# Decoder step: layer 1's window scores on fp32 tiles of 32 rows, values projected second, and the sample's mixing on 128 rows

## The chip, the cores and the metric

The kernel runs on one core of a Trainium2 chip. The metric is the device time of one execution in microseconds. Three runs of the kernel before took 1108.77, 1109.03 and 1109.35 us; their median is 1109.03.

## The reference

One inference step of a two-layer decoder for 256 prompt tokens and 8 sample sequences of 8 tokens, 320 tokens in all, with a model width of 1024. Layer 0 runs a gated MLP whose mixing matrix works along the positions, and a retention mixer. Layer 1 runs a sliding-window attention of 16 query heads on 4 key heads with RoPE and a learned sink for each head. Each layer then has a cross attention into 256 memory tokens and a squared-ReLU MLP. Cut to what the change touches:

```python
def sgu_mix(u, v, ln_g, ln_b, w_s, b_s):          # layer 0; c = 128 (prompt) or 8 (sample)
    vn = layer_norm(v, ln_g, ln_b)
    w = jnp.where(tril, w_s[:, :c, :c], 0)
    mixed = einsum('gts,bnsgd->bntgd', w, vn by chunks) + b_s[:, :c]
    return u * mixed

q, k, v = split(h @ w_qkv + b_qkv)                # layer 1; q and k through rotary
s = einsum('...qkgd,...skd->...kgqs', q, k) * 64 ** -0.5
s = where(valid, s, -inf)                         # 0 <= distance < 128
p = softmax(concatenate([s, sink]))[..., :-1]
o = einsum('...kgqs,...skd->...qkgd', p, v)
```

All is computed in float32.

## The kernel before

Activations are feature-major: 8 chunks of 128 features by 320 tokens. Weights stream from memory in tiles of 128 x 2048, in the order of a list, `_plan`. To keep float32 accuracy in the one-pass fp32r form of a matmul, weights and activations are split into a rounded high part and the rest: ScalarE makes `whi`, VectorE makes `wlo` (1024 columns each, four buffers), and `gemm2` runs three matmuls for each product: high by high, high by low, low by high. `gemm_tok` does the same with tokens as output rows, 48 matmuls and, for the sample, 16 more. The split of the weight after next is issued when a projection begins.

Work that isn't a projection is put between the matmuls of projections by hand: `hook(i, f, j=7)` runs `f` at step `j` of 16 of the i-th projection from now, and TensorE takes its instructions in that order. VectorE's and ScalarE's order comes from the scheduler of the framework.

Layer 1 before. The projection `w_qkv` has the groups 4 (keys), 0 to 3 (queries; a group holds one query head for each of the four key heads), and 5 (values, token-major). `qk_group` evicts a group: VectorE multiplies by the row scale and forms the four rotary products, POOL adds them into `QA`. A key head's half-heads lie on 32 of the 128 rows of `QA`. For scores the kernel stacks: `hilo` splits keys and queries into high and low parts, `stack_k` (into a tile tagged `k8b`) and `stack_q` (into one tagged `Z`) copy 32-row pieces so that one key head's high and low halves fill 128 rows, with 32 copies on VectorE and 32 on ScalarE. Each score block of one head is then two fp32r matmuls of 256 columns on the whole array, 64 in all.

The attention of the prompt is cut into 12 units, run by `slot`: `w1` (scores, masked maximum on VectorE, exponentials on ScalarE, normalising on VectorE), `w2f` (transposes) and `w3` (times values). Slots are hooked from the value projection on, through the four memory key projections (`mem1.mk`) and the memory value projections (`mem1.mv`); `ws_prep`, `ws_scores`, `ws_tr` and `ws_pv` do the sample's attention.

Layer 0's mixing: for each of 8 chunks the prompt's two blocks are matmuls with 128 rows, and the sample's is one with 64 rows, `VA[2]` (rows 0 to 63 of the tile `kb8`) by `wts`. Rows 64 to 127 of the same tile hold the retention values `VR[2]`; rows 64 to 127 of `wd_s` hold the retention's sample decay.

In the trace's names `mm` and `at` are PSUM banks of projections and of the rest, `k8b` and `Z` the stacked keys and queries (or `kb8` with `cst` in the mixing), `k` the tile `QA` (tag `k10`), `w` a scratch tile, `cst` the constants.

Of the kernel before, what the change touches and what calls it, by code (L numbers as in the profile page):

```python
# [9 lines left out]
F32 = mybir.dt.float32  # L10
F32R = mybir.dt.float32r
I32 = mybir.dt.int32
AF = mybir.ActivationFunctionType
ALU = mybir.AluOpType
# [3 lines left out]
P = 128  # L18
# [55 lines left out]
def decoder_step(ctx: ExitStack, tc: tile.TileContext, d, plan):  # L74
# [9 lines left out]
    def sb(shape, tag, bufs=1, dt=F32):  # L84
        cnt[0] += 1
        return pool.tile(list(shape), dt, tag=tag, bufs=bufs, name=f"{tag}_{cnt[0]}")

    def bank(kind="mm"):
        cnt[0] += 1
        return pmm.tile([P, 512], F32, tag=kind, bufs=4, name=f"{kind}_{cnt[0]}")  # L90
# [581 lines left out]
    def cec(name, i=0, n=None):  # L672
        o, w = CE[name]
        return ce[:, o + i:o + (w if n is None else i + n)]
# [45 lines left out]
    wt = cec("wt").rearrange("p (g t) -> p g t", g=4)  # L720
    wts = cec("wd_s")[:64].rearrange("p (g t) -> p g t", g=4)
    decs = cec("wd_s")[64:128]
    G.affine_select(out=wt, in_=wt, pattern=[[0, 4], [1, P]], compare_op=ALU.is_ge, fill=0.0,
# [11 lines left out]
    scT = [lnt[:, 2048:2560], k10[:, 2560:3072]]  # L735
    scS = kb8[64:128, 1024:1280]
    kz = [va[:, 2048:2560], vr[:, 2048:2560], kb8[64:128, 1280:1792]]
    qxi = cec("xi").rearrange("p (h t) -> p h t", h=4)
# [224 lines left out]
    for g in range(4):  # L963
        def evac(ps, i0=0, g=g):
            for i in range(len(ps)):
# [5 lines left out]
                for tb in range(2):  # L971
                    T.matmul(mp[:, tb * P:(tb + 1) * P], VA[tb][:, c * P:(c + 1) * P], wt[:, g], start=True, stop=True)
                T.matmul(mp[:, NPR:NT], VA[2][:, c * P:(c + 1) * P], wts[:, g], start=True, stop=True)
                mix = sb([P, NT], "t2", 1)
# [55 lines left out]
    bv = coc("bv")  # L1030
    khl = sb([P, 2, 4, 256], "k8b", 1, F32R)

    def qk_group(g):
# [16 lines left out]
        gemm2(("w_qkv", g), nm.h, nm.l, NT, evac)  # L1050

    def hilo(src, w):
        hi = sb([P, 512], "w2", W2, F32R)[:, :w]
        lo = sb([P, 512], "w2", W2, F32R)[:, :w]
        if len(src.shape) == 3:
            hi = hi.rearrange("p (g t) -> p g t", g=src.shape[1])
            lo = lo.rearrange("p (g t) -> p g t", g=src.shape[1])
        A.activation(hi, src, AF.Copy)
        V.tensor_tensor(lo, src, hi.bitcast(F32), op=ALU.subtract)
        return hi.bitcast(F32), lo.bitcast(F32)  # L1060

    def stack_k():
        for f in range(2):
            hl = hilo(QA[:, 8 + f, :NPR], NPR)
            for kv in range(4):
                r = slice(32 * kv, 32 * kv + 32)
                for x in range(2):
                    for du in range(2):
                        q = (f + 2 * du) * 32
                        if du:  # L1070
                            V.tensor_copy(khl[q:q + 32, x, kv], hl[x][r])
                        else:
                            A.activation(khl[q:q + 32, x, kv], hl[x][r], AF.Copy)

    sq_t = {}

    def stack_q(gp, fs=(0, 1)):
        if 0 in fs:
            sq = sb([P, 2080], "Z", 1, F32R)[:, :2048].rearrange("p (k g t) -> p k g t", k=4, g=2)
            sq_t[gp] = sq  # L1080
        sq = sq_t[gp]
        for f in fs:
            hl = hilo(QAv[:, 2 * gp:2 * gp + 2, f, :NPR], 512)
            for kv in range(4):
                r = slice(32 * kv, 32 * kv + 32)
                for x in range(2):
                    q = (f + 2 * x) * 32
                    if x:
                        V.tensor_copy(sq[q:q + 32, kv], hl[x][r])
                    else:  # L1090
                        A.activation(sq[q:q + 32, kv], hl[x][r], AF.Copy)

# [22 lines left out]

    units = []
    for gp in range(2):
        for pr in range(2):
            units.append((0, gp, pr, None))
        for kv in range(4):  # L1120
            units.append((1, gp, kv // 2, kv))
    us, up_, uo = {}, {}, {}

    def w1(u):
        n, gp, pr, kv = units[u]
        heads = [(k, g) for k in ((2 * pr, 2 * pr + 1) if n == 0 else (kv,)) for g in range(2)]
        nh = len(heads)
        kw = 512 // nh
        s = sb([P, 512], "w2", W2).rearrange("p (h k) -> p h k", k=kw)
        mx = sb([P, nh], "w_mx", 4)  # L1130
        msk = m1[:, P:256] if n == 0 else m1
        for j, (k, g) in enumerate(heads):
            if j % 2 == 0:
                sp = bank("at")
            o = (j % 2) * 256
            for x in range(2):
                T.matmul(sp[:, o:o + 256], sq_t[gp][:, k, g, n * P:(n + 1) * P], khl[:, x, k],
                         start=(x == 0), stop=(x == 1))
            V.tensor_tensor_reduce(out=s[:, j], in0=sp[:, o:o + kw], in1=msk, op0=ALU.add, op1=ALU.max,
                                   scale=1.0, scalar=NEG, accum_out=mx[:, j:j + 1])  # L1140
        sums = sb([P, nh], "w_sm", 4)
        if n == 0:
            for i in range(2):
                i0 = CV["sink_p"][0] - CV["sink_s"][0] + (2 * pr + i) * 4 + 2 * gp
                sink_softmax(s[:, 2 * i:2 * i + 2], 2, mx[:, 2 * i:2 * i + 2], nsink[:, i0:i0 + 2],
                             cvc("sink_p", (2 * pr + i) * 4 + 2 * gp, 2), sums[:, 2 * i:2 * i + 2], True)
        else:
            i0 = CV["sink_p"][0] - CV["sink_s"][0] + kv * 4 + 2 * gp
            sink_softmax(s, 2, mx, nsink[:, i0:i0 + 2], cvc("sink_p", kv * 4 + 2 * gp, 2), sums, True)
        us[u] = s  # L1150

    def w2f(u):
        n, gp, pr, kv = units[u]
        s = us.pop(u)
        tp = bank("at")
        pt = sb([P, 512], "w2", W2)
        for j in range(4):
            if n == 0:
                T.transpose(tp[:, j * P:(j + 1) * P], s[:, j], ident)
            else:  # L1160
                T.transpose(tp[:, j * P:(j + 1) * P], s[:, j % 2, (j // 2) * P:(j // 2 + 1) * P], ident)
        A.activation(pt, tp, AF.Copy)
        up_[u] = pt

    def w3(u):
        n, gp, pr, kv = units[u]
        pt = up_.pop(u)
        first = n == 0 or kv % 2 == 0
        if first:
            uo[n, gp, pr] = bank("at")  # L1170
        po = uo[n, gp, pr]
        for i in range(2):
            k = 2 * pr + i if n == 0 else kv
            ro = slice((k % 2) * 64, (k % 2) * 64 + 64)
            kb = 0 if n == 0 else i
            T.matmul(po[ro, :256], VW[:, kb, k * 64:(k + 1) * 64], pt[:, i * 256:(i + 1) * 256],
                     start=(n == 0 or i == 0), stop=(n == 0 or i == 1))
        if n == 0 or kv % 2 == 1:
            src = po[:, :256].rearrange("p (g q) -> p g q", g=2)
            c0 = pr * 4 + 2 * gp  # L1180
            oh = OH[:, c0:c0 + 2, n * P:(n + 1) * P]
            A.activation(oh, src, AF.Copy)
            V.tensor_tensor(OL[:, c0:c0 + 2, n * P:(n + 1) * P], src, oh.bitcast(F32), op=ALU.subtract)

# [82 lines left out]

    def slot(i):
        for u in (2 * i - 4, 2 * i - 3):
            if 0 <= u < 12:  # L1270
                w3(u)
        for u in (2 * i - 2, 2 * i - 1):
            if 0 <= u < 12:
                w2f(u)
        for u in (2 * i, 2 * i + 1):
            if u < 12:
                w1(u)

    def rows_out():
# [4 lines left out]

    qk_group(0)
    hook(0, stack_k)
    qk_group(1)
    hook(0, lambda: stack_q(0, (0,)))
    hook(1, lambda: stack_q(0, (1,)))
    qk_group(2)  # L1290
    qk_group(3)
    hook(0, lambda: slot(0))
    gemm_tok([("w_qkv", 5)], nm.h, nm.l, XS, 256, evac)
    hook(0, lambda: slot(1), rows_out)
    hook(1, lambda: slot(2), lambda: stack_q(1))
    hook(2, ws_prep, lambda: slot(3))
    hook(3, lambda: slot(4))
    for g in range(4):
        mem1.mk(g)
    hook(0, lambda: slot(5), lambda: ws_scores(0))  # L1300
    hook(1, lambda: slot(6), lambda: ws_scores(1))
    hook(2, lambda: slot(7), lambda: ws_tr(0))
    hook(3, lambda: ws_tr(1), j=3)
# [49 lines left out]
def _plan():  # L1353
# [35 lines left out]
    p += mo(0) + mlp(0)  # L1389
    p += [("w_qkv", 4), ("w_qkv", 0), ("w_qkv", 1), ("w_qkv", 2), ("w_qkv", 3), ("w_qkv", 5)]  # L1390
    p += [("w_mk", 1, g) for g in range(4)] + [("w_mv", 1, 0, 0), ("wk",), ("w_mv", 1, 0, 1), ("w_mv", 1, 1, 0),
# [205 lines left out]
```

## Time and profile before

| | |
|---|---|
| median of 3 runs | 1109.03 us |
| the profiled execution | 1110.15 us, span 1108.0, granted clock 0.995 |
| busy: PE, PEld | 1079.5 (97%), 1018.4 (92%) |
| busy: DVE, ACT, POOL | 716.3 (65%), 519.3 (47%), 98.8 (9%) |
| chain that ended last | PE 88%, DVE 6%, ACT 2%, DMA 2%, issue 1% |
| HBM traffic | 181 GB/s over the span |

PE is the matmul engine's streaming, PEld its weight loads, which overlap it. A matmul's drawn length includes its latency, so the distance between two starts tells its cost, not its length. The granted clock is in parts of full speed, and the stage of layer 1's projections and window attention lies from 607 to 725 us of the span.

### The profile page before, as it was taken

The page shows a single profiled execution, that of the slowest core. Times are in us where ns is not written, and L with a number is a line of the kernel's source. Part 1 is how long each engine was busy: PE and PEld are TensorE (multiplying, and loading weights), DVE is VectorE, ACT ScalarE, POOL GpSimd, SP SyncE. Part 2 cuts the span into 40 slices and gives each one's busy share as a digit, 9 for nine tenths or more (in the row PEclk, how much of TensorE's full clock was granted, in tenths as well). Part 3 has the DMA queues.
Part 4 walks back from the last instruction along what each step waited for, and adds up shares of the span by engine and source line. Part 5 has one row for each costly group of instructions (what it writes and reads, how often), then busy time and mean ns, then how long its engine had stood idle before and what let it go on. Part 6 is the DMA issues. An engine that isn't in the chain of part 4 may idle for free.

```text
span 1108.0 us, 18438 instructions
## 1 busy us (share of the span) xinstructions
PE 1079.5 (97%) x7424; PEld 1018.4 (92%) x7424; DVE 716.3 (65%) x1427; ACT 519.3 (47%) x894; POOL 98.8 (9%) x108
## 2 busy tenths in 40 slices
PE   7999999999999999999999979999999999999996
PEld 7888989999978999999999978889969999999995
DVE  8978866776545766454547998857445865555542
ACT  6455632654344555353436557645133554443432
POOL 4400000022000200000002131102000200000001
PEclk9999999999999999999999999999999999999998
DMA  9443358646777544444444334547587344444421
GB/s 340 158 146 124 134 190 283 235 143 234 295 294 307 224 149 153 152 153 152 153 153 153 122 114 158 175 164 277 198 309 283 120 150 150 153 153 153 152 76 48
DMA packets 30980, 201.53 MB, mean 182 GB/s; under 512 B 3624, under 2 KB 4792, under 8 KB 7992
## 3 DMA queue, kind: packets, MB, share of 16 engines
q1 hardware_dynamic: 27584, 187.13, 46.7%
q0 software_dynamic: 2512, 11.54, 2.9%
q10 hardware_dynamic: 800, 1.70, 0.5%
q8 instruction: 58, 0.95, 0.3%
q14 instruction: 26, 0.21, 0.1%
HBM read 187.51 MB, written 12.85 MB: 181 GB/s over the span
## 4 chain that ended last, share of the span: by engine, by line
PE 88%; DVE 6%; ACT 2%; DMA 2%; issue 1%; SPq 0%; ACTq 0%; DVEq 0%
PE mm L62 75%; PE at L62 13%; DVE wlo L62 2%; DMA stage<-ws 1%; DVE XL L62 1%; DVE t L62 1%; DVE w L62 1%; ACT whi L62 1%; DVE Z L62 0%; DVE X L62 0%; ACT XH L62 0%; DMA X<-x 0%; ACT w L62 0%; ACT Z L62 0%; ACT sqt L62 0%
## 5 line engine op out<-in xcount | busy, mean ns | idle before, releaser
L62 DVE TENSOR_TENSOR wlo<-stage,whi 128x1024 fp32r<-128x1024 f32 (+1 forms) x270 | 334.3, 1245 | 198.1 <-ACT whi L62 196.4
L62 ACT ACTIVATE whi<-stage 128x1024 fp32r<-128x1024 f32 (+1 forms) x270 | 280.2, 1051 | 380.2 <-PE mm L62 277.9
L62 PE MATMUL mm<-HH,whi 128*128 128x320 f32 (+1 forms) x960 | 293.7, 307 | 0.0
L62 PE MATMUL mm<-HL,whi 128*128 128x320 f32 (+1 forms) x960 | 293.0, 305 | 0.0
L62 PE MATMUL mm<-HH,wlo 128*128 128x320 f32 (+1 forms) x960 | 292.7, 305 | 0.0
L62 PE MATMUL mm<-XH,whi 128*128 128x320 f32 x912 | 286.4, 314 | 5.8 <-ACT whi L62 5.8
L62 PE MATMUL mm<-XH,wlo 128*128 128x320 f32 x912 | 283.0, 311 | 0.4 <-DVE wlo L62 0.4
L62 PE MATMUL mm<-XL,whi 128*128 128x320 f32 x912 | 282.9, 310 | 0.0
L62 PEld LDWEIGHTS mm<-HH,whi 128*128 128x128 f32 x960 | 180.1, 188 | 2.5 <-issue 1.6
L62 PEld LDWEIGHTS mm<-HL,whi 128*128 128x128 f32 x960 | 180.4, 188 | 0.4 <-DVE HL L62 0.3
L62 PEld LDWEIGHTS mm<-HH,wlo 128*128 128x128 f32 x960 | 180.3, 188 | 0.1
L62 PEld LDWEIGHTS mm<-XH,whi 128*128 128x128 f32 x912 | 172.3, 189 | 7.4 <-ACT whi L62 5.8
L62 PEld LDWEIGHTS mm<-XH,wlo 128*128 128x128 f32 x912 | 172.1, 189 | 0.9 <-DVE wlo L62 0.9
L62 PEld LDWEIGHTS mm<-XL,whi 128*128 128x128 f32 x912 | 172.4, 189 | 0.6
L62 POOL TENSOR_TENSOR ssq<-ssq,sqt 128x320 f32<-128x320 f32 x39 | 41.5, 1065 | 638.2 <-ACT sqt L62 637.2
L62 DVE TENSOR_TENSOR X<-mm,X 128x320 f32<-128x320 f32 x112 | 51.7, 488 | 57.7 <-PE mm L62 57.5
L62 DVE SCALAR_TENSOR_TENSOR t<-mm,RB 128x320 f32<-128x320 f32 x64 | 30.1, 490 | 25.5 <-PE mm L62 22.6
L62 DVE TENSOR_TENSOR HL<-t,HH 128x320 fp32r<-128x320 f32 x80 | 36.7, 485 | 10.5 <-ACT HH L62 9.9
L62 ACT ACTIVATE t<-t 128x320 f32<-128x320 f32 x80 | 34.0, 460 | 17.9 <-DVE t L62 17.9
L62 DVE SCALAR_TENSOR_TENSOR XL<-X,cv,XH 128x320 fp32r<-128x320 f32 x48 | 37.7, 808 | 4.5 <-ACT XH L62 4.5
L62 ACT ACTIVATE HH<-t 128x320 fp32r<-128x320 f32 x80 | 34.5, 462 | 11.2 <-DVE t L62 10.7
L62 ACT ACTIVATE XH<-X,cv 128x320 fp32r<-128x320 f32 x48 | 26.3, 554 | 20.6 <-DVE X L62 19.2
(232 smaller groups left out, 1076.7 us busy)
## 6 DMA issues: line engine op xcount, KB each, us to landing
stage<-ws SPq DMA_DIRECT2D x162, 1024.0 KB, 4.8
o_ret_s<-stage POOLq DMA_DIRECT2D x8, 512.0 KB, 6.1
HH<-ws SPq DMA_DIRECT2D x4, 1024.0 KB, 6.9
HL<-ws SPq DMA_DIRECT2D x4, 1024.0 KB, 6.6
k8a<-ws SPq DMA_DIRECT2D x2, 1024.0 KB, 8.8
o_mem_k<-k8a POOLq DMA_DIRECT2D x2, 1024.0 KB, 8.2
o_mem_v<-k8b POOLq DMA_DIRECT2D x2, 1024.0 KB, 11.2
cst<-ce SPq DMA_DIRECT2D x1, 1296.0 KB, 10.6
```

What stands on the lines that cost most here:

```text
L62: r = f(*a, **k)
```

## The change

It does three things. Layer 1's scores are taken from `QA` as it stands, in fp32: `w1` runs for each head and half-head four matmuls of 32 rows, one for each key head, into four PSUM banks, and then the softmax of all of them; `hilo`, `stack_k` and `stack_q` are gone. There are three batches in place of 12 units: second block with query heads 0 and 1, first block with all four, second block with 2 and 3, of 16, 32 and 16 matmuls. The values are projected right after the keys, ahead of the queries. The sample's mixing matmul runs over all 128 rows of `kb8`, with zeros in the lower half of `wts`, and the retention's decay gets a place and a load of its own.

```diff
-    wts = cec("wd_s")[:64].rearrange("p (g t) -> p g t", g=4)
-    decs = cec("wd_s")[64:128]
+    wts = cec("wd_s").rearrange("p (g t) -> p g t", g=4)
...
+    decs = kb8[64:128, 1792:2048]
+    S.dma_start(decs, d["dec_s"])
...
-                T.matmul(mp[:, NPR:NT], VA[2][:, c * P:(c + 1) * P], wts[:, g], start=True, stop=True)
+                T.matmul(mp[:, NPR:NT], kb8[:, c * P:(c + 1) * P], wts[:, g], start=True, stop=True)
...
-    def hilo(src, w):
-    def stack_k():
-    def stack_q(gp, fs=(0, 1)):
...
-            for x in range(2):
-                T.matmul(sp[:, o:o + 256], sq_t[gp][:, k, g, n * P:(n + 1) * P], khl[:, x, k],
-                         start=(x == 0), stop=(x == 1))
...
+    def w1(n, gp, tag):
+        gs = range(4) if n == 0 else (2 * gp, 2 * gp + 1)
+        kw = 512 // len(gs)
+        sp = [bank("at") for _ in range(4)]
+        for j, g in enumerate(gs):
+            for f in range(2):
+                for kv in range(4):
+                    r = slice(32 * kv, 32 * kv + 32)
+                    T.matmul(sp[kv][:, j * kw:(j + 1) * kw], QAv[r, g, f, n * P:(n + 1) * P], QA[r, 8 + f, :kw],
+                             start=(f == 0), stop=(f == 1))
+        big = sb([P, 2080 if tag == "Z" else 2048], tag)
...
+        for kv in range(4):
+            s = big[:, kv * 512:(kv + 1) * 512].rearrange("p (h k) -> p h k", k=kw)
...
+            sink_softmax(s, nh, mx, nsink[:, i0:i0 + nh], cvc("sink_p", kv * 4 + gs[0], nh), sums, True)
...
+        for kb in range(n + 1):
+            for i in range(2):
+                k = 2 * pr + i
+                T.matmul(po[i * 64:i * 64 + 64, :w], VW[:, kb, k * 64:(k + 1) * 64], pts[i][:, kb * w:(kb + 1) * w],
+                         start=(kb == 0), stop=(kb == n))
...
-    qk_group(0)
-    hook(0, stack_k)
-    qk_group(1)
-    hook(0, lambda: stack_q(0, (0,)))
-    hook(1, lambda: stack_q(0, (1,)))
-    qk_group(2)
-    qk_group(3)
-    hook(0, lambda: slot(0))
     gemm_tok([("w_qkv", 5)], nm.h, nm.l, XS, 256, evac)
-    hook(0, lambda: slot(1), rows_out)
-    hook(1, lambda: slot(2), lambda: stack_q(1))
-    hook(2, ws_prep, lambda: slot(3))
-    hook(3, lambda: slot(4))
+    hook(2, lambda: w1(1, 0, "k8b"), j=9)
+    hook(3, lambda: w2f(1, 0, 0), lambda: w2f(1, 0, 1), j=9)
+    hook(4, lambda: w3(1, 0, 0), lambda: w2f(1, 0, 2), lambda: w2f(1, 0, 3), rows_out, j=3)
+    hook(4, lambda: w1(0, 0, "Z"), j=13)
+    hook(5, lambda: w3(1, 0, 1), ws_prep, j=5)
+    hook(6, lambda: w2f(0, 0, 0), lambda: w2f(0, 0, 1), j=3)
+    hook(6, lambda: w3(0, 0, 0), lambda: w2f(0, 0, 2), lambda: w2f(0, 0, 3), j=13)
+    hook(7, lambda: w3(0, 0, 1), j=3)
+    hook(7, lambda: w1(1, 1, "k8b"), j=9)
+    for g in range(4):
+        qk_group(g)
     for g in range(4):
         mem1.mk(g)
...
-    p += [("w_qkv", 4), ("w_qkv", 0), ("w_qkv", 1), ("w_qkv", 2), ("w_qkv", 3), ("w_qkv", 5)]
+    p += [("w_qkv", 4), ("w_qkv", 5), ("w_qkv", 0), ("w_qkv", 1), ("w_qkv", 2), ("w_qkv", 3)]
...
-    w8[64:] = ce.pop("dec_s").reshape(64, 4, 64)
...
+        "dec_s": ce.pop("dec_s"),
```

Where the first scores stand on TensorE before: inside the value projection (`mm` from `whi`, `XH`), which follows query group 3. `x2` are the two matmuls of a head.

```order
L62 MATMUL mm_6594<-whi_6509,XH_5893 128x256
L62 MATMUL mm_6594<-wlo_6510,XH_5893 128x256
L62 MATMUL mm_6594<-whi_6509,XL_5894 128x256
L62 MATMUL at_6632<-k8b_6128,Z_6456 128x256 x2
L62 MATMUL at_6639<-k8b_6128,Z_6456 128x256 x2
L62 MATMUL at_6671<-k8b_6128,Z_6456 128x256 x2
L62 MATMUL at_6678<-k8b_6128,Z_6456 128x256 x2
L62 MATMUL mm_6593<-whi_6513,XH_5893 128x256
```

And in the change: behind 30 matmuls of query group 2. Each row is one fp32 matmul of 32 rows for another key head, from `QA` (`k`) alone, and three more such rounds of four follow.

```order
L62 MATMUL mm_6475<-XH_5894,whi_6396 128x320
L62 MATMUL mm_6475<-XL_5895,whi_6396 128x320
L62 MATMUL mm_6475<-XH_5894,wlo_6397 128x320
L62 MATMUL at_6506<-k_917_6128 128x256
L62 MATMUL at_6507<-k_917_6128 128x256
L62 MATMUL at_6508<-k_917_6128 128x256
L62 MATMUL at_6509<-k_917_6128 128x256
```

So the first scores moved from the value projection, then the last of the six, into query group 2, now the fifth of the six.

VectorE ahead of its first score rows (`ISA` is the masked maximum) before: the split of queries into `w`, a weight split, the copies into `Z`, and then the eviction of query group 3.

```order
L62 TENSOR_TENSOR w_995_6544<-k_917_6127,w_994_6543 128x512
L62 TENSOR_TENSOR wlo_6599<-stage_6596,whi_6598 128x1024
L62 CAST Z_6456<-w_995_6544 32x512 x4
L62 TENSOR_TENSOR t_996_6579<-mm_6517,RB_6240 128x320
L62 TENSOR_TENSOR t_997_6580<-mm_6518,RB_6240 128x320
L62 SCALAR_TENSOR_TENSOR t_998_6583<-t_996_6579,cv_62,cst_6122 128x320
L62 SCALAR_TENSOR_TENSOR t_999_6584<-t_997_6580,cv_62,cst_6122 128x320
L62 SCALAR_TENSOR_TENSOR t_1000_6588<-t_996_6579,cv_62,cst_6122 128x320
L62 TENSOR_TENSOR wlo_6603<-stage_6596,whi_6602 128x1024
L62 SCALAR_TENSOR_TENSOR t_1001_6589<-t_997_6580,cv_62,cst_6122 128x320
L62 ISA w_1010_6630,w_mx_6631<-at_6632,cst_6122 128x128
L62 ISA w_mx_6631 128x1
```

In the change there is no copy: the eviction of group 1 (`t`), two weight splits, and the maxima, which now write into the tile tagged `k8b`.

```order
L62 SCALAR_TENSOR_TENSOR t_972_6454<-t_970_6450,cv_62,cst_6123 128x320
L62 SCALAR_TENSOR_TENSOR t_973_6455<-t_971_6451,cv_62,cst_6123 128x320
L62 SCALAR_TENSOR_TENSOR t_974_6459<-t_970_6450,cv_62,cst_6123 128x320
L62 TENSOR_TENSOR wlo_6471<-stage_6464,whi_6470 128x1024
L62 SCALAR_TENSOR_TENSOR t_975_6460<-t_971_6451,cv_62,cst_6123 128x320
L62 TENSOR_TENSOR wlo_6622<-stage_6619,whi_6621 128x1024
L62 ISA k8b_6526,w_mx_6527<-at_6506,cst_6123 128x256
L62 ISA w_mx_6527 128x1
```

Behind group 1's eviction the maxima of a whole batch stand in one block, ahead of the eviction of group 2.

## Rows read from the trace of the kernel before

**Rows 1.** stretches of the layer 1 projections and window attention: busy us of each engine, granted clock:

```profile
640.00:660.00 20.00, 14.41 (x93) 13.71 (x93) 19.76 (x33) 9.27 (x13) 5.58 (x6) 0.91 0.29 106
...
sum 118.00, PE 110.19 PEld 102.45 DVE 105.62 ACT 74.50 POOL 23.39; mean PE 22.04 PEld 20.49 DVE 21.12 ACT 14.90 POOL 4.68
```

**Rows 2.** timeline of PE, 692 to 694 us (start, us, engine, operation, count):

```profile
692.76 1.46 PE L62 MATMUL at<-k8b,Z 128*128 128x256 f32 x10
694.05 0.28 PE L62 MATMUL mm<-HH,whi 128*128 128x256 f32 x1
694.17 0.27 PE L62 MATMUL mm<-HL,whi 128*128 128x256 f32 x1
```

**Rows 3.** timeline of PE around the first scores, with idle time and its releaser:

```profile
653.73 2.12 PE L62 MATMUL at<-k8b,Z 128*128 128x256 f32 x8 [3.83 <-DVE Z L62]
655.65 0.41 PE L62 MATMUL mm<-whi,XH 128*128 128x256 f32 x1
655.87 0.41 PE L62 MATMUL mm<-wlo,XH 128*128 128x256 f32 x1
...
659.79 0.39 PE L62 MATMUL at<-k8b,Z 128*128 128x256 f32 x1 [1.10 <-DVE w_mx L62]
```

**Rows 4.** timeline of PE, three later waits of the stage:

```profile
646.81 0.35 PE L62 MATMUL mm<-whi,XH 128*128 128x256 f32 x1 [0.66 <-DVE t L62]
...
670.45 0.51 PE L62 MATMUL at<-k8b,Z 128*128 128x256 f32 x2 [1.06 <-DVE w_mx L62]
...
691.40 0.48 PE L62 MATMUL at<-k8b,Z 128*128 128x256 f32 x2 [0.91 <-DVE Z L62]
```

**Rows 5.** timeline of DVE ahead of the first scores:

```profile
651.26 1.87 DVE L62 TENSOR_TENSOR wlo<-stage,whi 128x1024 fp32r<-128x1024 f32 x1
653.17 1.78 DVE L62 CAST Z<-w 32x512 fp32r<-32x512 f32 x4
```

**Rows 6.** groups of DVE from 607 to 726 us: the copies into stacked tiles (count | busy, mean ns):

```profile
L62 DVE CAST Z<-w 32x512 fp32r<-32x512 f32 x16 | 6.7, 420 | 0.4
...
L62 DVE CAST k8b<-w 32x256 fp32r<-32x256 f32 x16 | 4.5, 319 | 0.1
```

**Rows 7.** PE, fp32 on the whole array: a group of the span, and the timeline at 712 us:

```profile
L62 PE MATMUL at<-k8a,k 128*128 128x256 f32 x64 | 15.4, 386 | 0.4 <-ACT w L62 0.4
...
712.78 0.66 PE L62 MATMUL at<-stage,XH 128*128 128x128 f32 x4
713.28 0.56 PE L62 MATMUL at<-k,XH 128*128 128x64 f32 x4
713.68 0.55 PE L62 MATMUL at<-stage,XH 128*128 128x128 f32 x3
```

**Rows 8.** PE, column tiles: the timeline at 146 us, and weight loads from 140 to 150:

```profile
146.09 1.07 PE L62 MATMUL at<-stage,Z 128*32 128x256 f32 x16
147.09 0.75 PE L62 MATMUL at<-k8a,w 128*128 128x256 f32 x4
...
L62 PEld LDWEIGHTS at<-cst,HH 128*128 128x128 f32 x4 | 0.6, 190 | 0.0
...
L62 PEld LDWEIGHTS at<-stage,Z 128*32 128x32 f32 x16 | 0.4, 109 | 0.6 <-issue 0.4
```

**Rows 9.** timeline of PE: the sample's mixing pair on 64 rows:

```profile
117.05 0.43 PE L62 MATMUL at<-cst,k8b 64*128 64x64 f32 x2
117.41 0.71 PE L62 MATMUL at<-cst,HH 128*128 128x128 f32 x4
```

**Rows 10.** timeline, all engines: the end of a query group and its rotation:

```profile
645.69 0.31 PE L62 MATMUL mm<-XL,whi 128*128 128x320 f32 x1
...
645.84 0.31 PE L62 MATMUL mm<-XH,wlo 128*128 128x320 f32 x1
646.18 0.89 DVE L62 TENSOR_TENSOR t<-mm,RB 128x320 f32<-128x320 f32 x2
...
650.82 1.24 POOL L62 TENSOR_TENSOR k<-t,t 128x320 f32<-128x320 f32 x1 [1.62 <-DVE t L62]
```

More of the change, by code (lines that the diff above doesn't have):

```diff
@@ L1030, in decoder_step @@
     bv = coc("bv")
-    khl = sb([P, 2, 4, 256], "k8b", 1, F32R)
     def qk_group(g):
@@ L1050, in qk_group @@
         gemm2(("w_qkv", g), nm.h, nm.l, NT, evac)
-    def hilo(src, w):
[L1053 to L1060, printed above, removed]
-    def stack_k():
[L1063 to L1066, printed above, removed]
-                for x in range(2):
[L1068 to L1075, printed above, removed]
-    def stack_q(gp, fs=(0, 1)):
[L1078 to L1091, printed above, removed]
     isc = 0.125
@@ L1114, in sink_softmax @@
             V.tensor_scalar(s[:, h], s[:, h], sums[:, h:h + 1], None, op0=ALU.mult)
[L1116 to L1119, printed above, removed]
-        for kv in range(4):
[L1121 to L1136, printed above, removed]
-                T.matmul(sp[:, o:o + 256], sq_t[gp][:, k, g, n * P:(n + 1) * P], khl[:, x, k],
-                         start=(x == 0), stop=(x == 1))
[L1139 to L1150, printed above, removed]
@@ L1152, in w2f @@
-    def w2f(u):
-        n, gp, pr, kv = units[u]
-        s = us.pop(u)
+    us, up_, uo = {}, {}, {}
+    def w1(n, gp, tag):
[9 more added lines that the diff above has]
+        big = sb([P, 2080 if tag == "Z" else 2048], tag)
+        msk = m1[:, P:256] if n == 0 else m1
+        nh = len(gs)
+        for kv in range(4):
+            s = big[:, kv * 512:(kv + 1) * 512].rearrange("p (h k) -> p h k", k=kw)
+            mx = sb([P, nh], "w_mx", 4)
+            for j in range(nh):
+                V.tensor_tensor_reduce(out=s[:, j], in0=sp[kv][:, j * kw:(j + 1) * kw], in1=msk, op0=ALU.add,
+                                       op1=ALU.max, scale=1.0, scalar=NEG, accum_out=mx[:, j:j + 1])
+            sums = sb([P, nh], "w_sm", 4)
+            i0 = CV["sink_p"][0] - CV["sink_s"][0] + kv * 4 + gs[0]
+            sink_softmax(s, nh, mx, nsink[:, i0:i0 + nh], cvc("sink_p", kv * 4 + gs[0], nh), sums, True)
+            us[n, gp, kv] = s
@@ L1155, in w2f @@
+    def w2f(n, gp, kv):
+        s = us.pop((n, gp, kv))
         tp = bank("at")
@@ L1162, in w2f, with w3 @@
         A.activation(pt, tp, AF.Copy)
[L1163 to L1183, printed above, removed]
+        up_[n, gp, kv] = pt
+    def w3(n, gp, pr):
+        po = bank("at")
+        ng = 4 if n == 0 else 2
+        w = ng * P
+        pts = [up_.pop((n, gp, 2 * pr + i)) for i in range(2)]
+        for kb in range(n + 1):
[3 more added lines that the diff above has]
+                         start=(kb == 0), stop=(kb == n))
+        src = po[:, :w].rearrange("p (g q) -> p g q", g=ng)
+        c0 = pr * 4 + 2 * gp
+        oh = OH[:, c0:c0 + ng, n * P:(n + 1) * P]
+        A.activation(oh, src, AF.Copy)
+        V.tensor_tensor(OL[:, c0:c0 + ng, n * P:(n + 1) * P], src, oh.bitcast(F32), op=ALU.subtract)
     sm_ = {}
@@ L1266, in evac @@
         V.scalar_tensor_tensor(VW[64:128, 2], fs, nm.rs[64:128, 2:3], bv[64:128], op0=ALU.mult, op1=ALU.add)
[L1268 to L1277, printed above, removed]
     def rows_out():
@@ L1283, in rows_out @@
         G.dma_start(d["wv_n"], VW[64:128, 2])
-    qk_group(0)
-    hook(0, stack_k)
-    qk_group(1)
-    hook(0, lambda: stack_q(0, (0,)))
-    hook(1, lambda: stack_q(0, (1,)))
-    qk_group(2)
-    qk_group(3)
-    hook(0, lambda: slot(0))
-    gemm_tok([("w_qkv", 5)], nm.h, nm.l, XS, 256, evac)
-    hook(0, lambda: slot(1), rows_out)
-    hook(1, lambda: slot(2), lambda: stack_q(1))
-    hook(2, ws_prep, lambda: slot(3))
-    hook(3, lambda: slot(4))
+    gemm_tok([("w_qkv", 5)], nm.h, nm.l, XS, 256, evac)
+    hook(2, lambda: w1(1, 0, "k8b"), j=9)
[9 more added lines that the diff above has]
+        qk_group(g)
     for g in range(4):
         mem1.mk(g)
-    hook(0, lambda: slot(5), lambda: ws_scores(0))
-    hook(1, lambda: slot(6), lambda: ws_scores(1))
-    hook(2, lambda: slot(7), lambda: ws_tr(0))
+    hook(0, lambda: ws_scores(0), j=5)
+    hook(1, lambda: w2f(1, 1, 0), lambda: w2f(1, 1, 1), j=1)
+    hook(1, lambda: w3(1, 1, 0), lambda: w2f(1, 1, 2), lambda: w2f(1, 1, 3), lambda: ws_scores(1), j=9)
+    hook(2, lambda: w3(1, 1, 1), lambda: ws_tr(0))
     hook(3, lambda: ws_tr(1), j=3)
```

## Prediction

> **What bounds the kernel now.** I read the page's chain first: by the table above TensorE holds 88% of it, so a microsecond is won only where TensorE stands idle, runs at the low clock, or streams something that can be streamed in less time. The table by stretches then says where that is. From 607 to 725 us, the layer 1 projections and window attention, TensorE is busy for 110.19 of 118 us while VectorE is busy for 105.62, and the stretch 640 to 660 has a granted clock of 0.91 [rows 1]. Everywhere else the waits of TensorE are small, so I went through this stage matmul by matmul.
>
> The timeline of TensorE shows the stalls. Plain matmuls of 256 columns start 0.12 us apart (694.05 to 694.17), though each is drawn 0.28 us long [rows 2]. Ahead of the first scores TensorE idles 3.83 us for VectorE's copies into the stacked query tile; the 8 scores that follow take 1.92 us (653.73 to 655.65) instead of 8 x 0.12, and 8 matmuls behind them start 0.22 us apart [rows 3]. That is 256 columns at 1.2 GHz and not at 2.4: the idle time cost the clock as well. Four more waits stand in the stage: 1.10 behind the first, and 0.66, 1.06 and 0.91 us, all for VectorE [rows 3, 4]. The reason stands in VectorE's own order: the copies that the first scores wait for begin at 653.17, behind a weight split of 1.87 us and without a gap [rows 5].
>
> **The change part by part.** *Stalls that lose their cause.* The five idle times sum to 3.83 + 1.10 + 0.66 + 1.06 + 0.91 = 7.56 us. An idle time is counted from the drawn end (0.28) and not from the next possible start (0.12), so each hides 0.16 more: 8.4 us. The 8 slow plain matmuls add 8 x 0.10 = 0.8. The change deletes the copies behind them: 32 on VectorE, 6.7 and 4.5 us busy [rows 6], with as many on ScalarE and the six hi/lo splits ahead of them. VectorE loses at least 11.2 of 105.62 us, so the order that made it late is gone.
>
> *The old scores.* 64 matmuls: 8 in 1.92 us, the other 56 at the pace of the ten at 692.76, 1.29 / 10 = 0.13 us, so 7.2. Removed: 9.1 us [rows 2, 3].
>
> *The new scores.* The operands are now fp32 and not fp32r, and an fp32 matmul of the program is two records in the trace: the 32 score matmuls of the two cross attentions stand there as 64 [rows 7]. So 16 + 32 + 16 = 64 matmuls are 128 records, 64 of 256 columns and 64 of 128. On the whole array such a record takes 15.4 / 64 = 0.24 us for 256 columns and 0.125 for 128 (712.78 to 713.28, four) [rows 7]. Run singly that would be 23 us; all depends on whether four tiles of 32 rows run side by side. No row tile has a neighbour in this trace. Column tiles do: 16 records of 128 rows by 32 columns, with 256 columns streamed, take 1.00 us, 0.0625 each, so four ran at once and one tile took 0.25 per record [rows 8]. A column tile's load has 32 columns and lasts 109 ns, a row tile's has 128; a load of 128 columns lasts 190 [rows 8]. If a tile doesn't hide its own load, a record costs 0.25 + 0.081 = 0.33 per tile, 0.083 with four tiles, and 0.10 less per tile, or 0.058, for 128 columns. 64 x 0.083 + 64 x 0.058 = 9.0 us. Low end: loads cost nothing more than the column tiles' own, 64 x 0.0625 + 64 x 0.0375 = 6.4. High end with overlap: one load at a time. The records of 64 columns (713.28 to 713.68, 0.10 each) are shorter streams than their loads and give that pace [rows 7]: 128 x 0.10 = 12.8. I take 9.0, because the half-height pair below behaves like a tile that waits for its own loads.
>
> There is a rule against this change here. The Trainium skill, "TensorE: Matmul & The Clock Gate", section on LDWEIGHTS, says that a load of 32 rows by 128 columns takes as long as one of 128 by 128, its columns divided by 1.2 GHz. The 190 ns against 109 agree that columns count. By the page's figure, as an estimate, 128 loads one after another are 13.7 us, and the sum below would end near 1105.
>
> *Drains.* The sample's 64-row pair takes 0.36 us (117.05 to 117.41) for two records of 64 columns that on the full array take 0.10 each [rows 9, 7]: a visit to another tile height costs some 0.16 us. Three batches of scores are three visits; with four tiles to fill I take 0.3 each, 0.9 in all (0.5 to 1.5).
>
> *The sample's mixing on 128 rows.* Eight such pairs now stay in the full array: 0.36 - 0.20 = 0.16 each, 1.3 us, in a stage where TensorE has no wait of note. The lower 64 rows of the weight tile are zero, so they add nothing. Between no gain and 2 us, since the matmuls around it could also lose a refill. The new 64 KB load stands in SP's queue behind a weight load and well ahead of its reader; nothing waits for it. POOL's select covers 128 rows and not 64; it is off the path.
>
> *The second-place value projection.* Its 64 matmuls are the same. It fills the time in which VectorE makes the norm's row scale, and its own results now come long before attention wants them. No cost.
>
> *What is late next.* The first batch stands behind 30 of the 48 matmuls of query group 2, at 0.15 us each some 4.4 us after the group before it ends. In the kernel before, a group's last rotation ends on POOL at 652.06, 5.9 us after VectorE began on it at 646.18 [rows 10]. The batch begins with group 0's 16 records, 1.3 us, and has 8 records of group 1's first half after them, so the last quarter of it is reached about when POOL is done. The transposes stand 7 us and more behind each batch; VectorE needs for a batch some 8 us beside the 6 us of a projection's evictions and splits, so it falls behind by about that, and catches up over the memory projections. I charge 1.0 us of new waits (0 to 3) over three batches. The normalised scores, transposes and value matmuls are the same in number and streamed columns; I cost them at nothing.
>
> **Sum.** 8.4 + 0.8 + 9.1 + 1.3 - 9.0 - 0.9 - 1.0 = 8.7 us gained. The profiled execution took 1110.15 us (span 1108.0); the sum was made in it and would bring it to 1101.5. It stands 1.1 above the median of the runs, 1109.03, so the forecast for the median is **1100.3**. With the low price of scores and drains and no new waits the gain is 12.7 us (1096.3); with the high prices (12.8, 1.5, 3.0 and no gain in mixing) it is 1.0 (1108.0), but these don't come together: the dear loads alone make 4.9 (1104.1).
>
> **The rivals.** *Loads in single file.* The scores take 12.8 us: 1104.1. For it: all loads have 128 columns, and the 64-column records show loads setting the pace [rows 7]. Against: the tiles' rows are disjoint. *VectorE stays the late one.* The whole of a batch's softmax arrives at once, between the evictions of a projection; if the transposes or a weight split then wait as long as today, the 8.4 us come back less the 1.0 I charge: 1107.7. For it: VectorE is still at some 90 of 108 us. *The other side: row tiles do not overlap.* Then 128 records run singly, 23 us with hidden loads, 64 x 0.33 + 64 x 0.23 = 36 without: 1114 to 1127, slower. It decides from 17.7 us for the scores, 0.14 per record. For it: no two row tiles run together in this trace, and the pair of 64 rows pays for its loads. Against: column tiles overlap fourfold [rows 8], and each key head has a PSUM bank of its own. *The change doesn't do what it says*, the stalls being owed to the weight splits alone: then they move and only 9.1 - 9.9 + 1.3 remains, about no change.
>
> **How the numbers follow.** The forecast's own pace 0.52 (1097.5 to 1102.5); loads that hide better, down to 1096, 0.12; single file 0.18; VectorE late 0.08; no overlap 0.07; doesn't do what it says 0.03. The range 1095.5 to 1106 takes the first three. A measurement of this kernel can tell about 0.2%, 2.2 us, from no change. Faster by more than that: the first three and a part of the late VectorE, 0.86; within it 0.07; slower 0.07.
>
> **What would show it.** In the new profile the stretch from 607 us should be about 7 us shorter, without an idle time over 1 us ahead of scores, with a clock of 1.00 throughout; records of a 32-row tile should start about 0.06 to 0.08 us apart; mixing records of 64 columns about 0.10. Records 0.10 apart whatever their columns mean single file; 0.2 and more mean no overlap. A long wait for VectorE ahead of a transpose or of a memory projection means that the load moved and did not go.

## The result and the profile after

The changed kernel takes 1095.62 us (median, 1094.03 to 1096.85) against 1109.19 for the kernel before: ratio 0.9875, 95% interval 0.9863 to 0.9886. The gain is 13.6 us where 8.7 were forecast; 0.9875 of 1109.03 is 1095.2, just under the low end of the range (1095.5). The direction and the mechanism held, the size of the gain did not. The profiled execution has a span of 1094.4 us against 1108.0.

The page of the changed kernel, the first rows of its parts 1 and 4, shows that TensorE is still what bounds:

```profile
PE 1072.5 (98%) x7480; PEld 1011.3 (92%) x7480; DVE 695.1 (64%) x1371; ACT 498.3 (46%) x850; POOL 103.3 (9%) x108
...
PE 84%; DVE 7%; DMA 5%; ACT 2%; issue 1%; POOL 1%; SPq 0%; ACTq 0%; DVEq 0%
```

The same view by stretches as [rows 1] (us, then busy us of PE, PEld, DVE, ACT, POOL with counts, granted clock, DMA share, GB/s), now for the changed kernel:

```profile
640.00:660.00 20.00, 20.00 (x166) 18.74 (x165) 18.69 (x57) 11.51 (x30) 8.77 (x6) 1.00 0.30 106
660.00:680.00 20.00, 19.06 (x200) 17.01 (x199) 16.38 (x76) 12.61 (x45) 6.78 (x11) 1.00 0.35 112
607.00:715.00 108.00, 107.06 (x848) 97.98 (x846) 85.07 (x255) 56.24 (x143) 27.32 (x28) 1.00 0.46 155
```

TensorE is busy for 107.06 of 108 us, VectorE for 85.07 instead of 105.62 of 118, and the clock of 0.91 has become 1.00. TensorE's timeline of the changed kernel shows all of the new scores, with the one wait that is left:

```profile
641.64 0.31 PE L62 MATMUL mm<-XH,wlo 128*128 128x320 f32 x1
641.88 2.01 PE L62 MATMUL at<-k 32*128 32x256 f32 x32
643.82 0.41 PE L62 MATMUL mm<-XH,whi 128*128 128x320 f32 x1
...
661.59 1.84 PE L62 MATMUL at<-k 32*128 32x128 f32 x56
664.37 0.50 PE L62 MATMUL at<-k 32*128 32x128 f32 x8 [0.94 <-POOL k L62]
664.80 0.39 PE L62 MATMUL mm<-HH,whi 128*128 128x256 f32 x1
...
685.99 2.01 PE L62 MATMUL at<-k 32*128 32x256 f32 x32
```

32 records of 256 columns take 1.94 us (641.88 to 643.82), 0.061 each, so four row tiles do run side by side. The 3.83 us ahead of scores [rows 3] and the four waits behind it [rows 3, 4] are gone; 0.94 us for POOL's rotation of the last query group is new. The weight loads, as the group of PEld from 607 to 732 us has them (busy us, mean ns | idle before), overlap each other:

```profile
L62 PEld LDWEIGHTS at<-k 32*128 32x128 f32 x128 | 5.0, 185 | 1.7 <-POOL k L62 1.1 <-issue 0.2
```

128 loads of 185 ns are 23.7 us one after another, yet PEld is busy with them for 5.0.

Where the time went is read from one landmark to the next, the last rows of the norm ahead of the stage and the first of the output projection behind it. Kernel before:

```profile
614.81 0.72 PE L62 MATMUL at<-ones,ssq 128*128 128x1 f32 x6
...
745.23 0.31 PE L62 MATMUL mm<-HH,whi 128*128 128x320 f32 x1
```

Changed kernel:

```profile
612.61 0.72 PE L62 MATMUL at<-ones,ssq 128*128 128x1 f32 x6
...
731.48 0.31 PE L62 MATMUL mm<-HH,whi 128*128 128x320 f32 x1
```

The stage takes 118.9 us instead of 130.4: 11.5 won here. The other 2.2 stand ahead of it (614.81 against 612.61). The sample's mixing lies there, from the first mixing records to the first plain matmul behind the last. Its timeline now begins and ends so:

```profile
116.43 0.61 PE L62 MATMUL at<-cst,HH 128*128 128x128 f32 x4
116.88 0.33 PE L62 MATMUL at<-cst,k8b 128*128 128x64 f32 x2
117.05 0.66 PE L62 MATMUL at<-cst,HH 128*128 128x128 f32 x4
117.55 0.33 PE L62 MATMUL at<-cst,k8b 128*128 128x64 f32 x2
117.69 0.39 PE L62 MATMUL mm<-XH,whi 128*128 128x320 f32 x1
...
150.80 0.40 PE L62 MATMUL mm<-HH,whi 128*128 128x320 f32 x1
```

In the kernel before, the first records, the second pair with the next plain matmul, and the end stand here:

```profile
116.52 0.61 PE L62 MATMUL at<-cst,HH 128*128 128x128 f32 x4
...
118.06 0.43 PE L62 MATMUL at<-cst,k8b 64*128 64x64 f32 x2
118.42 0.42 PE L62 MATMUL mm<-XH,whi 128*128 128x320 f32 x1
...
153.52 0.42 PE L62 MATMUL mm<-HH,whi 128*128 128x320 f32 x1
```

The pair takes 0.17 us where [rows 9] has 0.36, and the four records behind it 0.50 (117.05 to 117.55) where they took 0.65 (117.41 to 118.06). So a visit to 64 rows cost 0.19 inside and 0.15 behind it, where more mixing follows. The eight visits with what lies between take 34.37 us (116.43 to 150.80) instead of 37.00 (116.52 to 153.52), with the same other matmuls: 2.6 us, 0.33 a visit. The landmark's 2.2 is less sure: from the mixing's end to the norm the same matmuls take 461.3 us in the kernel before and 461.8 in the changed one, and from 459.2 to 461.8 over all traces below.

### The profile page after: what moved, and what is told of

The parts are those of the page before. It is cut to its first block, busy times and chain, and to the rows that moved or that the text cites. A ratio compares the mean times of both kernels' runs of the same rounds, so it can differ in the third digit from the quotient of the medians.

```text
span 1094.4 us, 18448 instructions
## 1 busy us (share of the span) xinstructions
PE 1072.5 (98%) x7480; PEld 1011.3 (92%) x7480; DVE 695.1 (64%) x1371; ACT 498.3 (46%) x850; POOL 103.3 (9%) x108
## 4 chain that ended last, share of the span: by engine, by line
PE 84%; DVE 7%; DMA 5%; ACT 2%; issue 1%; POOL 1%; SPq 0%; ACTq 0%; DVEq 0%
PE mm L62 74%; PE at L62 10%; DMA stage<-ws 5%; DVE wlo L62 3%; ACT whi L62 1%; DVE XL L62 1%; DVE t L62 1%; DVE X L62 0%; ACT XH L62 0%; DVE k8b L62 0%; DMA X<-x 0%; DVE Z L62 0%; POOL k L62 0%; POOL XH L62 0%; ACT sqt L62 0%
## 5 line engine op out<-in xcount | busy, mean ns | idle before, releaser
L62 DVE TENSOR_TENSOR wlo<-stage,whi 128x1024 fp32r<-128x1024 f32 (+1 forms) x270 | 330.5, 1233 | 200.8 <-ACT whi L62 199.2
```

The lines of the kernel that those rows point to most:

```text
L62: r = f(*a, **k)
```

## The experiments

Three sets of kernels, each with the kernel before (1109.11, 1108.47 and 1108.74 us) on the same chip; the changed kernel went with the second and third as `changed_again` (1094.45 us, ratio 0.9874 [0.9857, 0.989]) and `changed_thrice`.

**Do the tiles overlap because their matmuls alternate?** `tiles_in_turn` only moves the loop over key heads outward, so that each tile's matmuls follow one another:

```diff
-        for j, g in enumerate(gs):
-            for f in range(2):
-                for kv in range(4):
+        for kv in range(4):
+            for j, g in enumerate(gs):
+                for f in range(2):
```

> The changed kernel with the same 64 score matmuls in another order: key head outermost, so that neighbours on TensorE use the same 32-row tile. Theory A (four tiles run side by side, and each hides its loads): neighbours now queue, a record costs 0.23 us for 256 columns and 0.125 for 128, 64 of each make 22.7 us in place of some 6, so about 16 us more than the changed kernel, 1112. If a tile can't hide its own load: 0.33 and 0.23, 36 us, about 1125. Rival (the tiles' neighbours don't matter, a record of 32 rows is simply cheap): no change, 1095 to 1096.

Measured: 1108.04 us, ratio 0.9988 [0.9979, 0.9997]. Nearly the whole gain is lost, though less than with loads that nothing hides. Its TensorE timeline, its loads and its stretch:

```profile
640.33 4.91 PE L62 MATMUL at<-k 32*128 32x256 f32 x32
645.17 0.41 PE L62 MATMUL mm<-XH,whi 128*128 128x320 f32 x1
...
669.95 0.41 PE L62 MATMUL mm<-HL,whi 128*128 128x256 f32 x1
670.16 0.41 PE L62 MATMUL mm<-HH,wlo 128*128 128x256 f32 x1
```

```profile
L62 PEld LDWEIGHTS at<-k 32*128 32x128 f32 x128 | 14.7, 187 | 1.2 <-issue 0.2
```

```profile
660.00:680.00 20.00, 20.00 (x165) 18.98 (x164) 15.82 (x75) 11.41 (x42) 4.91 (x9) 0.91 0.30 107
```

The batch takes 4.84 us instead of 1.94, 0.151 a record, and PEld is busy for 14.7 us instead of 5.0: the loads of one tile in this batch start 0.22 us apart, where the changed kernel's loads of four tiles start within 0.02 us of each other. Behind the second batch (6.6 us, a tile at a time) 11 plain matmuls start 0.21 us apart, the pace of 1.2 GHz, though TensorE had not waited: the clock was lost as well. Of the 12.1 us that the stage takes longer than in `changed_again`, 9.5 are the scores', 1.3 the plain matmuls' at this clock, and most of the rest is a later wait of 1.1 us for ScalarE.

The starts of single records say two things more. Within one tile records of 256 columns start 0.216 us apart and those of 128 columns 0.112, not the 0.33 and 0.23 of a tile that waits for its own loads. And where one tile hands over to the next, records of the two tiles alternate for some 0.75 us at 0.11 each, so two run at once; therefore the 32 records take 4.84 us and not 32 x 0.216 = 6.9, and the expected 16 us were too many.

**What does one more record cost?** `scores_twice` writes every score matmul a second time with the same result:

```diff
-        for j, g in enumerate(gs):
+        for j, g in [(j, g) for _ in range(2) for j, g in enumerate(gs)]:
```

> The changed kernel with every score matmul issued twice into the same place; the result is the same. This prices the 128 records without the way in and out of the tiles. Theory A with hidden loads (64 x 0.0606 + 64 x 0.029): 5.7 us more than the changed kernel, less the 1 us in which the first-block batch waits for POOL today. With loads that a tile waits for, as the prediction took them: 9.0 us more.

Measured: 1100.67 us, ratio 0.9927 [0.9911, 0.9944]; 6.2 us above `changed_again` by the medians, 5.2 in the stage of the profiled executions. Its timeline of TensorE:

```profile
639.42 3.74 PE L62 MATMUL at<-k 32*128 32x256 f32 x64
643.08 0.41 PE L62 MATMUL mm<-XH,whi 128*128 128x320 f32 x1
...
663.37 2.29 PE L62 MATMUL at<-k 32*128 32x128 f32 x72 [0.67 <-POOL k L62]
665.59 0.39 PE L62 MATMUL mm<-HH,whi 128*128 128x256 f32 x1
```

64 records of 256 columns take 3.66 us and 32 took 1.94: 32 more cost 1.72, or 0.054 each. Behind the wait 72 records of 128 columns take 2.22 and 8 took 0.43 (664.37 to 664.80): 64 more cost 1.79, or 0.028. So 64 of each are 64 x 0.054 + 64 x 0.028 = 5.2 us, and a batch has some 0.2 us on top that doesn't grow with it.

**The mixing alone.** `mixing_only` is the kernel before with this:

```diff
-    wts = cec("wd_s")[:64].rearrange("p (g t) -> p g t", g=4)
-    decs = cec("wd_s")[64:128]
+    wts = cec("wd_s").rearrange("p (g t) -> p g t", g=4)
...
+    decs = kb8[64:128, 1792:2048]
+    S.dma_start(decs, d["dec_s"])
...
-                T.matmul(mp[:, NPR:NT], VA[2][:, c * P:(c + 1) * P], wts[:, g], start=True, stop=True)
+                T.matmul(mp[:, NPR:NT], kb8[:, c * P:(c + 1) * P], wts[:, g], start=True, stop=True)
```

> The kernel before with nothing changed but the sample's mixing on 128 rows and the decay's own load. By the lead that the trace of the changed kernel has when the mixing is over, 2.3 us faster than before (1106.9 against 1109.2). By the price in the prediction 1.3. If that lead comes from another part of the change, nothing.

Measured: 1106.2 us, ratio 0.9972 [0.9959, 0.9986], a gain of 2.9 us with bounds of 1.5 and 4.5. All of the stage's stalls stand as before (its waits ahead of scores are 3.82, 1.35, 1.07 and 0.94 us) and the stage takes 130.4 us again. From the first mixing records to the first plain matmul behind the last its trace has 34.36 us, as the changed kernel's 34.37. The prediction's 1.3 lies under the interval; the 2.6 of these rows lies in it.

**The place of the scores.** `later_slots` is the kernel before with every slot of scores, transposes and values one projection later, the copies kept:

```diff
-    hook(0, lambda: slot(0))
     gemm_tok([("w_qkv", 5)], nm.h, nm.l, XS, 256, evac)
-    hook(0, lambda: slot(1), rows_out)
-    hook(1, lambda: slot(2), lambda: stack_q(1))
+    hook(0, lambda: slot(0), rows_out)
+    hook(1, lambda: slot(1))
+    hook(2, ws_prep, lambda: slot(2), lambda: stack_q(1))
...
```

> The kernel before with every slot of window attention one projection later, nothing else changed; stacking and copies stay. Theory B (the stalls come from where the scores stand, not from how they are computed): the waits of TensorE, 8.4 us, and the 1.7 us at the low clock go, about 1099 to 1101. Theory C (the copies make VectorE late wherever the scores stand): the waits come back elsewhere, 1106 to 1110.

Measured: 1108.86 us, ratio 0.9994 [0.9985, 1.0004]: no gain. The first slot of scores is no longer late. The second waits, as TensorE's timeline and then VectorE's show:

```profile
662.25 2.07 PE L62 MATMUL at<-k8b,Z 128*128 128x256 f32 x8 [4.84 <-DVE w_mx L62]
```

```profile
658.25 2.45 DVE L62 TENSOR_TENSOR wlo<-stage,whi 128x1024 fp32r<-128x1024 f32 x2
...
661.90 0.29 DVE L62 CUSTOM_DVE_ANT_0 w<-at,cst 128x128 f32<-128x128 f32 x1
```

The banks that the second slot needs are read out by a reduction that VectorE begins at 661.90, behind weight splits of 2.45 us and the sample's fold. The waits of the stage sum to 0.67 + 0.30 + 0.43 + 4.84 + 0.45 = 6.7 us against 7.56 [rows 3, 4].

**The place of the values.** `values_last` is the changed kernel with the value projection behind the query groups, as it was, and the attention's places moved by one for it:

```diff
-    gemm_tok([("w_qkv", 5)], nm.h, nm.l, XS, 256, evac)
...
     for g in range(4):
         qk_group(g)
+    gemm_tok([("w_qkv", 5)], nm.h, nm.l, XS, 256, evac)
```

> The changed kernel with the values projected last again, and attention's later steps one projection later to match. Theory A: the place of that projection carries nothing, within 1 us of the changed kernel (1095 to 1097). Rival (the early value projection is what gives VectorE its slack): waits of 2 us and more ahead of the first scores or the transposes, 1098 and up.

Measured: 1093.36 us, ratio 0.9858 [0.9845, 0.9872]; its stage takes 118.5 us, that of `changed_again` 118.6. The order of the projections carries nothing that these runs can tell.

**VectorE's amount or the scores' waiting?** `copies_back` is the changed kernel with the deleted splits and copies at their old places, written into tiles that nobody reads, so that no matmul waits for the copies' values; `copies_twice` has them twice. The hooks, without the bodies of `back_k` and `back_q`:

```diff
...
+    hook(1, back_k)
+    hook(2, lambda: back_q(0, (0,)))
+    hook(3, lambda: back_q(0, (1,)))
+    hook(5, lambda: back_q(1))
     for g in range(4):
         qk_group(g)
```

> The changed kernel with the deleted work of VectorE and ScalarE put back at its old places (the six hi/lo splits, 32 copies on VectorE and as many on ScalarE), into tiles that nobody reads; the scores and TensorE's order stay as changed. VectorE was busy for 85 of the 108 us from 607 in the changed kernel and gets back the 11.2 us of copies and the splits, so about 100. Theory A, the stalls went because VectorE has less to do: with the work back the evictions and softmax come late again and 4 to 8 us of TensorE's waits return, 1099 to 1103 us. Theory B, the stalls came from the scores' own waiting for the copies, and for the reductions between pieces of two banks, which the change cut: nothing on TensorE waits for the work put back, and the time is that of the changed kernel plus 0 to 2 us, 1095 to 1097.

> As the run with the deleted work put back, but all of it twice (the copies into tiles that nobody reads). VectorE would then have some 115 us of work for a stretch of 108. Theory A: 10 us or more above the changed kernel, 1105 or more. Theory B: VectorE itself is over-full by some 7 us there, of which the memory projections behind can take a part, so 2 to 7 us, 1097 to 1102. If it costs under 2 us the stage has more slack on VectorE than the busy time says.

Measured: `copies_back` 1104.11 us, ratio 0.9972 [0.9957, 0.9987], 10.3 us above `changed_thrice` (1093.81, 0.9864 [0.9851, 0.9877]) and above what either theory gave it; `copies_twice` 1124.38, 1.0148 [1.0133, 1.0163], 30.6 above. Waits in the timeline of `copies_back`:

```profile
641.36 0.71 PE L62 MATMUL at<-k 32*128 32x256 f32 x8 [0.69 <-POOL k L62]
644.23 1.24 PE L62 MATMUL at<-k 32*128 32x256 f32 x8 [2.16 <-POOL k L62]
645.83 0.47 PE L62 MATMUL mm<-XL,whi 128*128 128x320 f32 x1
646.10 0.47 PE L62 MATMUL mm<-XH,wlo 128*128 128x320 f32 x1
...
667.28 1.82 PE L62 MATMUL at<-k 32*128 32x128 f32 x50 [1.45 <-DVE HL L62]
669.66 0.50 PE L62 MATMUL at<-k 32*128 32x128 f32 x8 [0.56 <-POOL k L62]
...
675.48 1.08 PE L62 MATMUL at<-w,cst 128*64 128x256 f32 x8 [2.28 <-DVE w_mx L62]
```

```profile
640.00:660.00 20.00, 17.15 (x120) 15.48 (x114) 19.58 (x62) 15.70 (x36) 4.33 (x4) 0.83 0.15 53
660.00:680.00 20.00, 15.71 (x171) 13.88 (x168) 18.75 (x70) 14.03 (x38) 11.23 (x12) 1.00 0.30 107
```

VectorE's own order there, ahead of the first maximum of the first batch:

```profile
647.38 2.24 DVE L62 CAST Z<-w 32x512 fp32r<-32x512 f32 x5
649.63 0.42 DVE L62 CUSTOM_DVE_ANT_0 k8b<-at,cst 128x256 f32<-128x256 f32 x1
```

The new waits are 7.1 us against the one of 0.68 in `changed_thrice`, and matmuls of 320 columns start 0.27 us apart (645.83 to 646.10), not 0.147: a granted clock of 0.83. POOL is named three times; ahead of the first two it rotates what VectorE has just handed it, and the third rotation stands behind copies of POOL's own. The stage takes 128.9 us instead of 118.6. So work that no matmul reads stalls TensorE, and the stalls are not only the scores' waiting for their own copies. The run does not separate the amount of that work from its place in VectorE's order: the copies stand directly ahead of the maxima. ScalarE's share of it came back too, but no new wait of TensorE names ScalarE.

**Fewer tile heights.** `fewer_heights` is the changed kernel with the sample's values and the sample's retention matmuls on 128 rows, the added rows zeroed once, and the second batch of scores two steps (six matmuls) later:

```diff
+    G.memset(kb8[0:64, 1024:1280], 0.0)
...
+    G.memset(VW[0:64, 2], 0.0)
...
-            T.matmul(po.rearrange("p (b x) -> p b x", b=8), VW[64:128, 2, pr * P:(pr + 1) * P],
+            T.matmul(po.rearrange("p (b x) -> p b x", b=8), VW[:, 2, pr * P:(pr + 1) * P],
...
-    hook(4, lambda: w1(0, 0, "Z"), j=13)
+    hook(4, lambda: w1(0, 0, "Z"), j=15)
```

> The changed kernel with two more of its 64-row matmuls carried over to 128 rows with zeros (the retention's inner product of the sample, and the new keys' values in the sample's window attention), and the first-block scores two steps later, to miss the 0.9 us wait for POOL. If a change of tile height costs 0.15 us each way, as the mixing shows: 0.3 for the first, 0.6 for the second, with the wait 1.8 us less than the changed kernel, about 1093.8. If the heights cost nothing here: 0.9 less or nothing.

Measured: 1094.23 us, ratio 0.9871 [0.9856, 0.9885], 0.2 us under `changed_again`: not to be told from none. The sample's values in the changed kernel, and then in this one:

```profile
724.18 1.12 PE L62 MATMUL at<-k,cst 64*128 64x512 f32 x2
725.23 2.00 PE L62 MATMUL at<-XL,stage 128*128 128x64 f32 x16
727.16 1.12 PE L62 MATMUL at<-k,cst 64*128 64x512 f32 x2
```

```profile
723.27 1.02 PE L62 MATMUL at<-k,cst 128*128 128x512 f32 x2
724.13 1.89 PE L62 MATMUL at<-XL,stage 128*128 128x64 f32 x16
725.86 1.08 PE L62 MATMUL at<-k,cst 128*128 128x512 f32 x2
```

A visit costs 2.59 us instead of 2.98, and two save 0.7 from there to the output projection (40.60 us from the first memory values against 41.31). The later batch gives it back, as this row of the same kernel shows:

```profile
664.23 0.50 PE L62 MATMUL at<-k 32*128 32x128 f32 x8 [1.28 <-POOL k L62]
```

The wait for POOL grew from 0.67 to 1.28 us although its reader came later: POOL's two rotations ahead of it took 2.25 and 1.93 us where they took 1.12 and 0.86 in `changed_again`. Why the same instruction has such different lengths isn't settled here. The retention part shows no gain: its records lie among the mixing, and from the first mixing records to the first plain matmul behind the last this kernel takes 34.37 us, `changed_again` 34.36. They fill only 64 of the array's columns either way, so they change the shape of the tile with 128 rows too; that this is why nothing was won is not shown.

**The parts that helped, together.** `last_and_full` is `values_last` with the first batch two steps later (`j=11` for `j=9`) and the sample's values on 128 rows, without the retention part and without the move of the second batch.

> The changed kernel with three edits that the other runs speak for: values projected last; the first batch of scores two column steps later (6 matmuls, 0.9 us), which should remove its 0.59 us wait for POOL; and the sample's values matmuls on 128 rows with zeros in place of 64 rows, whose stretch was 0.7 us shorter in the run that had it. Against the run with values last, 1093.4 us, that is 0.7 + 0.6 less: 1092.1. If POOL's rotations only come later too, as in the run with fewer tile heights, 1092.7. Against the changed kernel on the same chip 1.5 to 3 us less; if within 1 us the three carry nothing that can be measured.

Measured: 1092.24 us, ratio 0.9853 [0.9838, 0.9867], against 1093.81 for `changed_thrice` beside it. The 1.6 us are under what a measurement can tell; in the traces the stage takes 116.9 us against 118.6. No wait of TensorE is left in it: the second batch reads

```profile
659.80 2.07 PE L62 MATMUL at<-k 32*128 32x128 f32 x64
```

## Why the prediction was right, and where it was wrong

Term by term, in us of gain. Measured values come from the starts of TensorE's rows between the landmarks, the plain matmuls, scores and others summed apart:

| term | forecast | measured |
|---|---|---|
| stalls and cold matmuls gone | 8.4 + 0.8 | 9.7 (plain matmuls 92.5 to 83.4, and 0.6 of the switches that these now carry) |
| old scores | 9.1 | 9.7 |
| new scores, records | -9.0 | -5.2 (`scores_twice`) |
| drains, three batches | -0.9 | -1.2 (0.2 in a batch, 0.1 ahead, 0.1 behind) |
| new waits | -1.0 | -1.2 (0.94 drawn, and what its drawn end hides) |
| mixing | 1.3 | 2.6 |
| sum | 8.7 | 14.4; the landmarks give 11.5 + 2.2 = 13.7 |

*The stalls: right, and for the reason given.* VectorE loses its work and with it the order that made it late; all five waits are gone with the clock's loss, and nothing of size took their place. `copies_back` is the test: the same work without a reader costs 10.3 us. The rival "VectorE stays the late one" fails by the changed kernel's own trace, where no wait names VectorE, and "the change doesn't do what it says" by `copies_back`, where the waits return with the work. How much the larger batches add to this, no run splits. The margin is small: from 640 to 680 us VectorE is busy for 18.69 + 16.38 = 35.1 of 40 us in the changed kernel (35.7 in `changed_thrice`) and for 19.58 + 18.75 = 38.3 in `copies_back`.

*The failed step is the price of the new scores:* "If a tile doesn't hide its own load, a record costs 0.25 + 0.081 = 0.33 per tile, 0.083 with four tiles, and 0.10 less per tile, or 0.058, for 128 columns. 64 x 0.083 + 64 x 0.058 = 9.0 us." The records cost 0.054 and 0.028. No load shows in the time of a record, not even where one tile works alone (0.216 and 0.112 in `tiles_in_turn`), and even the low end of 6.4 was too dear. The choice of 9.0 over 6.4 rested on "the half-height pair below behaves like a tile that waits for its own loads". That pair was misread: it is slow because the array changes to another tile height and back, and not, as far as the runs show, because of its loads. The records behind the pair gain too when it goes, and `scores_twice` shows that a batch pays some 0.2 us once, whatever its length. How the 0.19 us inside the pair divide, no run shows.

*The same misreading cost the mixing term.* The prediction counted only what stood inside the pair, 0.16 us, and left out what its neighbours lose; for a batch of scores it took 0.3. Eight times 0.3 are 2.4; 2.6 were measured. These two terms are 3.8 + 1.3 of the 5 us missed. The other terms missed by 0.6 at most, and by 0.6 together.

*Loads in single file* was worth 0.18 and is excluded: the 128 loads keep PEld busy for 5.0 us. The Trainium skill, "TensorE: Matmul & The Clock Gate", section on LDWEIGHTS, prices a load by its columns. The 185 ns for 32 rows agree with the 190 ns of 128 rows [rows 8]; only the estimate of 13.7 us from it, which put the loads one after another, does not fit. *Row tiles don't overlap* is excluded by 0.061 us a record, far under its 0.14; `tiles_in_turn` shows the condition: written in turn, records of 256 columns cost 0.151 and nearly all of the gain goes.

The value projection and its place cost nothing, as forecast (`values_last`). The stretch was to shrink by about 7 us and shrank by 11.5; a wait over 1 us ahead of scores did not come (0.94).

## What to carry to other kernels

Before pricing an operation by an odd record in the trace, look at its neighbours: where they lose time as well, suspect a switch that is paid once per visit and that a batch dilutes. Row tiles are worth their switch when consecutive matmuls go to different tiles. An engine busy for nine tenths of a stretch that hands operands to the bounding engine can stall it with work that nobody waits for: put the deleted work back without a reader, and the trace shows what the deletion was worth.

## What the runs showed of the hardware

Loads of different row tiles overlap: 128 loads of 185 ns kept PEld busy for 5.0 us when matmuls alternated over four tiles, and for 14.7 when each tile had its turn. The Trainium skill, "TensorEngine Tiling (Array Packing)", Key Properties, says that different tiles can load weights and multiply in parallel, and that a change of tiling mode drains TensorE. Both agree with these traces, which add the price: 0.3 to 0.4 us for a visit and the way back (mixing 2.6 / 8, the sample's values 2.98 - 2.59, a batch of scores 0.4).

In `tiles_in_turn` the granted clock was 0.50, the level of 1.2 GHz, from 669 to 672 us (0.91 over the stretch), at the end of and behind the 6.6 us in which row tiles worked one after another and TensorE was never drawn idle. Behind its two batches of 4.84 us, and with four tiles alternating, it stayed at 1.00; the reason is not shown.
